# Sparse attention's queries computed with features as rows, their rotary partners fetched by transfers within SBUF, first weight tiles in halves, new shares

## The chip, the cores and the metric

The kernel runs on one core of one Trainium2 chip. The metric is the device time of one launch in microseconds (us). Before the change three runs gave a median of 1074.1 us (1072.49 to 1074.27).

## The reference, cut to what matters

Six stages follow one another on 256 tokens of 1024 features in fp32: a feed-forward network (FFN), a hybrid mixer, two FFNs, sparse attention (NSA) and a last FFN. The change touches the start of the first FFN and the projections at the head of the NSA.

```python
def swiglu(x, w_in, w_out):
    gate, up = jnp.split(x @ w_in, 2, axis=-1)
    ...

def nsa_mixer(x, positions, w_in, cmp_pos, cmp_w1, cmp_w2, w_out):
    proj = x @ w_in
    ...
    q, k_c, v_c, k_s, v_s, k_w, v_w, gates = jnp.split(proj, [int(s) for s in np.cumsum(sizes)], axis=-1)
    q = q.reshape(bsz, t_len, h, dk)
    ...
    q_rot = partial_rope(q, positions)
    k_s = partial_rope(k_s, positions)
    k_w = partial_rope(k_w, positions)
    ...
    k_cmp = compress_blocks(k_c, cmp_idx, cmp_pos[0], cmp_w1[0], cmp_w2[0])
    v_cmp = compress_blocks(v_c, cmp_idx, cmp_pos[1], cmp_w1[1], cmp_w2[1])
    ...
    s_cmp = jnp.einsum('bqged,bcgd->bgeqc', qg, k_cmp) * scale
    s_sel = jnp.einsum('bqged,bgqmd->bgeqm', qrg, k_sel) * scale
    s_win = jnp.einsum('bqged,bkgd->bgeqk', qrg, kw) * scale
    ...
    return o @ w_out
```

There are 16 heads of 64 features; the turn takes the first 16. `s_cmp` uses the plain queries, `s_sel` and `s_win` the turned ones. The rotary turn pairs feature d with feature d + 8 for d in 0 to 7 of each head: the first becomes x1 cos - x2 sin, the second x2 cos + x1 sin.

## The kernel before

**Products.** Each fp32 factor is split into a rounded half `hi` and a remainder `lo`, and each product is three matmuls (hi·hi, hi·lo, lo·hi; `mm3`). A weight tile arrives as `raw` (128x1024, 512 KB) by a DMA of the SP queue (`arrive`, L681). `split` (L672) writes `whi`, on ACT or DVE, and `wlo = raw - whi`, always on DVE. `col_tiles` (L709) gives tiles with 128 output features and all 8 blocks of 128 input features; `row_tiles` (L713) gives tiles with 512 output features and 2 input blocks.

**The order.** The program first lists all operations. `Plan.order` (L360) then sets the order on the engines by a model of their times, with each operation's place in the list as its priority; every engine works through its queue in that order. All instructions are issued by one line (L574), so the tiles' names tell them apart. In the NSA four strands are woven by `W_NSA` (L60, L2154): `attention`, `dense`, `compressed` and `out_g0`; the numbers set how fast each strand advances in the list.

**The NSA's head.** Token blocks b (2 of 128) and head groups g (2 of 8 heads). `dense` (L1930) does, for b = 0 and 1: keys, values and gates (`kv`), for b = 1 the compression's projections (`compress_in`, L1951: products `ps<-x,whi`, copies to `F`, sums to `X`), then `queries(0, wq, [b])`, then `keys(b)`, which splits the turned keys to `kd`; at the end come the queries of g = 1 for both blocks.

**The queries before** (L1885). For each g and b 24 matmuls `ps<-whi,x` or `ps<-wlo,x` of 512 columns give 128 tokens by 512 features. ACT copies them to `q`. Four fp32 transposes on PE (`mp<-ident,q`), with a copy, give the plain `qT`. `rope` turns `q` by six small operations on POOL or DVE. Four more transposes bring the turned queries to PSUM, from where `qs` is split in 64-row pieces (two CAST and two TENSOR_TENSOR on DVE for each g and b). `attend` (L2040) uses `qs`: scores `kd,qs`, the row maxima (TENSOR_REDUCE), `Exp` on ACT to `P`, a scaling of `P` (one half on DVE, one on ACT in eight pieces), transposes `mp<-ident,P`, copies to `PT`, products with `vtok`. `cmp_probs` uses `qT`. `compress` multiplies `X` by weights that are used unsplit (`mp<-raw,X`).

**The start** (`first_loads` L729, `first_steps` L1045). The tokens arrive in four DMAs of 256 KB: the first (block b = 0, first 4 input blocks) on the ACT queue, the others on SP. Weight tile 0 comes in two halves, the others whole. PE runs two warming calls on `ones`, then the products, four input blocks for b = 0 and then for b = 1.

Of the kernel before, what the change touches and what calls it, by code (L numbers as in the profile page):

```python
# [10 lines left out]
F32R = mybir.dt.float32r  # L11
# [48 lines left out]
W_HYB, W_NSA = (63.0, 66.0, 28.0, 29.0, 10.0), (81.0, 59.0, 103.0, 17.0)  # L60
# [9 lines left out]
HARD = False  # L70


def H3(t, h):
    return t.rearrange("p (h t) -> p h t", h=h)
# [118 lines left out]
class Plan:  # L193
# [83 lines left out]
    def price(self, op, eng, fn, args, kw):  # L277
# [15 lines left out]
        if fn == "dma_start":  # L293
            return {"sync": 60.0, "scalar": 400.0}.get(eng, 1100.0)
# [303 lines left out]
class K:  # L598
# [130 lines left out]
    def first_loads(self, x, w):  # L729

        nc = self.nc
        raws = []
        for n in range(8):
            raw = self.m4(1024, "raw", "W")
            if n % 2 == 0 and n < 4:
                self.first_tokens(x, n)
            for cs in [slice(0, 512), slice(512, 1024)] if n == 0 else [slice(0, 1024)]:
                nc.sync.dma_start(raw[:, cs], w[n][:, cs])
            if n % 2 and n < 4:
                self.first_tokens(x, n)  # L740
            raws.append(raw)
        return raws

    def first_tokens(self, x, n):

        queue = self.nc.sync if n else self.nc.scalar
        queue.dma_start(x[1][n // 2][:, n % 2], self.i['x_cols'][n].rearrange("p (k t) -> p k t", k=4))

    def first_weights(self, raw, parts):

        hi, lo = (self.m4(1024, name, "W", F32R) for name in ("whi", "wlo"))
        for cs in parts:
            self.split(hi[:, cs], lo[:, cs], raw[:, cs])
        return [(hi[:, k * 512:k * 512 + 512], lo[:, k * 512:k * 512 + 512]) for k in range(2)]
# [290 lines left out]
    def first_steps(self, x, w_in, gtiles, gts):  # L1045
# [6 lines left out]
        for c0, tag in ((0, "acc"), (DFF, "ps")):  # L1052
            both = [self.bank(tag) for b in range(2)]
            banks.append(both)
            w = []
            for n in range(4):
                for ks, hi, lo in self.halves(x, n % 2, n // 2) if c0 == 0 and n % 2 == 0 else []:
                    self.split(hi, lo, x[1][n // 2][:, n % 2, ks])
                w += self.first_weights(raws.pop(0), [slice(0, 1024)] if c0 or n > 1 else [slice(0, 512), slice(512, 1024)])
                for ks, hi, lo in self.halves(x, n % 2, n // 2) if c0 == 0 and n % 2 else []:  # L1060
                    self.split(hi, lo, x[1][n // 2][:, n % 2, ks])
            for k0 in range(0, KD, 4):
                for b in range(2):
# [736 lines left out]

    def tt(self, out, a, b, op):
# [16 lines left out]
    def nsa(self, x, then):  # L1818
# [3 lines left out]
        w_in = i['nsa_w_tok']  # L1822
# [58 lines left out]
        q = [self.m4(1024, f"q{b}") for b in range(2)]  # L1881
        qT = [H3(self.m4(1024, f"qT{b}"), 8) for b in range(2)]
        qs = [[H3(self.m4(1024, f"qs{b}{g}", dtype=F32R), 8) for g in range(2)] for b in range(2)]

        def queries(g, w, bs):  # L1885
            gs = slice(g * 512, (g + 1) * 512)
            for b in bs:
                ps = self.bank("ps")
                for k in range(KD):
                    self.mm3(ps, self.xb(x, b, k), w[k], k == 0, k == KD - 1)  # L1890
                    yield
                nc.scalar.activation(q[b][:, gs], ps, AF.Copy, scale=0.125)
                yield
# [5 lines left out]
                yield  # L1899
                pt = self.bank("mp")  # L1900
                for c in range(4):
                    nc.tensor.transpose(pt[:, c * P:(c + 1) * P], q[b][:, g * 512 + c * P:g * 512 + (c + 1) * P], self.ident)
                s = qs[b][g].rearrange("p (c two) t -> p c two t", two=2)
                up, dn = slice(0, 64), slice(64, 128)
                for e, (hi, lo) in enumerate(((up, dn), (dn, up))):
                    src = H3(pt, 4)[hi]
                    self.copy(s[hi, :, e, :], src)
                    V.tensor_tensor(s[lo, :, e, :], src, s[hi, :, e, :].bitcast(F32), OP.subtract)
                done.add(("q", g, b))
        kd = [self.m4(1024, f"kd{n}", dtype=F32R).rearrange("p (g r t) -> p g r t", g=2, r=2) for n in range(2)]  # L1910
# [11 lines left out]
        wq = self.row_tiles([w_in[n] for n in range(4)], 2)  # L1922
        wc = []
        done = set()
# [364 lines left out]
```

## Time and profile before

| what | us |
|---|---|
| median of three runs | 1074.1 |
| the profiled execution | 1073.94 |
| its span, first to last instruction | 1072.2 |
| the NSA's part of the span, about | 766 to 890 |
| the first product of the first FFN | 5.98 |

The profile's page gives the busy time of the engines and the chain that ended last. Its views group instructions by line and tile, give the waits of an engine, the chain in order of time, the timeline, and the busy time of each engine in chosen stretches. In a row such as `PE MATMUL mp<-ident,P`, `mp` is written and the others are read; for matmuls the tile named first is either factor. A time in brackets is the idle time ahead of a row and what ended it.

### The profile page before, as it was taken

The page shows a single profiled execution, that of the slowest core. Times are in us where ns is not written, and L with a number is a line of the kernel's source. Part 1 is how long each engine was busy: PE and PEld are TensorE (multiplying, and loading weights), DVE is VectorE, ACT ScalarE, POOL GpSimd, SP SyncE. Part 2 cuts the span into 40 slices and gives each one's busy share as a digit, 9 for nine tenths or more (in the row PEclk, how much of TensorE's full clock was granted, in tenths as well). Part 3 has the DMA queues.
Part 4 walks back from the last instruction along what each step waited for, and adds up shares of the span by engine and source line. Part 5 has one row for each costly group of instructions (what it writes and reads, how often), then busy time and mean ns, then how long its engine had stood idle before and what let it go on. Part 6 is the DMA issues. An engine that isn't in the chain of part 4 may idle for free.

```text
span 1072.2 us, 16134 instructions
## 1 busy us (share of the span) xinstructions
PE 1060.2 (99%) x5924; PEld 887.9 (83%) x5924; DVE 1010.4 (94%) x1440; ACT 724.1 (68%) x1155; POOL 76.6 (7%) x125
## 2 busy tenths in 40 slices
PE   9999999999999999999999999999999999999997
PEld 6888888898999888888888888888887778888886
DVE  6999999889969999999999999999988989999996
ACT  6678866489726766577766676677565877667770
POOL 1000000001002120000000000000011000000000
PEclk9999999999999999999999999999999999999999
DMA  9688868535515665478777647778552436467861
GB/s 367 226 274 235 254 219 289 166 131 186 182 41 179 199 232 177 142 251 244 203 240 272 225 144 237 234 248 254 204 217 67 151 114 219 151 222 236 261 191 39
DMA packets 65535, 217.79 MB, mean 203 GB/s; under 512 B 8576, under 2 KB 12336, under 8 KB 65456
## 3 DMA queue, kind: packets, MB, share of 16 engines
q1 hardware_dynamic: 60992, 200.77, 53.1%
q0 software_dynamic: 4320, 15.73, 8.2%
q8 instruction: 46, 0.75, 0.3%
q14 instruction: 33, 0.27, 0.1%
q10 hardware_dynamic: 144, 0.26, 0.1%
HBM read 213.96 MB, written 1.07 MB: 201 GB/s over the span
## 4 chain that ended last, share of the span: by engine, by line
PE 90%; DVE 6%; ACT 2%; DMA 1%; issue 1%; DVEq 0%; ACTq 0%
PE ps L574 42%; PE acc L574 33%; PE mp L574 15%; DVE wlo L574 2%; DVE arena L574 1%; DVE cv L574 1%; ACT whi L574 1%; DVE AT L574 0%; DMA raw<-in_hyb_w_tok_dram 0%; DMA X<-in_x_cols_dram 0%; DMA raw<-in_nsa_w_one_dram 0%; DVE P L574 0%; ACT cv L574 0%; DVE h L574 0%; DVE qs L574 0%
## 5 line engine op out<-in xcount | busy, mean ns | idle before, releaser
L574 DVE TENSOR_TENSOR wlo<-raw,whi 128x1024 fp32r<-128x1024 f32 (+3 forms) x417 | 490.0, 1206 | 9.9 <-ACT whi L574 8.7
L574 ACT ACTIVATE whi<-raw 128x1024 fp32r<-128x1024 f32 (+2 forms) x431 | 431.3, 1047 | 73.4 <-DVE raw L574 65.3
L574 PE MATMUL ps<-whi,x 128*128 128x512 f32 (+1 forms) x864 | 233.4, 387 | 0.0
L574 PEld LDWEIGHTS ps<-whi,x 128*128 128x128 f32 x864 | 157.2, 188 | 28.3
L574 DVE TENSOR_TENSOR raw<-raw,raw 128x1024 f32<-128x1024 f32 x128 | 152.3, 1215 | 0.0
L574 PE MATMUL ps<-wlo,x 128*128 128x512 f32 (+1 forms) x432 | 129.5, 387 | 0.0
L574 PE MATMUL ps<-x,whi 128*128 128x256 f32 (+2 forms) x560 | 115.3, 312 | 0.3 <-ACT cv L574 0.2
L574 PE MATMUL acc<-whi,gh 128*128 128x512 f32 x253 | 98.3, 392 | 0.0
L574 PE MATMUL acc<-whi,gl 128*128 128x512 f32 x253 | 98.1, 390 | 0.1
L574 PEld LDWEIGHTS ps<-x,whi 128*128 128x128 f32 (+1 forms) x560 | 90.3, 188 | 9.3 <-ACT cv L574 2.7
L574 PEld LDWEIGHTS ps<-wlo,x 128*128 128x128 f32 x432 | 79.4, 188 | 14.2 <-DVE wlo L574 0.2
L574 PE MATMUL acc<-wlo,gh 128*128 128x512 f32 x253 | 84.8, 392 | 0.0
L574 PE MATMUL ps<-x,wlo 128*128 128x256 f32 (+1 forms) x344 | 80.2, 286 | 0.0
L574 PE MATMUL acc<-whi,x 128*128 128x512 f32 x224 | 75.2, 411 | 1.1 <-ACT whi L574 1.1
L574 POOL DMA_DIRECT2D wlo<-in_ffn_w_out_dram x30 | 26.2, 873 | 558.7 <-ACT wlo L574 321.9
L574 PE MATMUL acc<-whi,g 128*128 128x512 f32 x192 | 61.2, 393 | 0.0
L574 PEld LDWEIGHTS ps<-x,wlo 128*128 128x128 f32 (+1 forms) x344 | 58.0, 189 | 1.7 <-DVE wlo L574 0.4
L574 PEld LDWEIGHTS acc<-whi,gl 128*128 128x128 f32 x253 | 47.4, 188 | 10.2 <-DVE gl L574 0.5
L574 PEld LDWEIGHTS acc<-whi,gh 128*128 128x128 f32 x253 | 47.4, 188 | 9.9 <-ACT gh L574 0.2
L574 PEld LDWEIGHTS acc<-wlo,gh 128*128 128x128 f32 x253 | 47.4, 188 | 9.7
L574 PEld LDWEIGHTS acc<-whi,x 128*128 128x128 f32 x224 | 42.3, 193 | 10.9 <-ACT whi L574 2.7
L574 PE MATMUL ps<-whi,fhi 128*128 128x512 f32 x128 | 50.0, 390 | 0.0
(287 smaller groups left out, 1722.5 us busy)
## 6 DMA issues: line engine op xcount, KB each, us to landing
raw<-in_ffn_w_in_dram SPq DMA_DIRECT2D x175, 512.0 KB, 5.3
raw<-in_ffn_w_out_dram SPq DMA_DIRECT2D x88, 512.0 KB, 4.0
wlo<-in_ffn_w_out_dram POOLq DMA_DIRECT2D x30, 512.0 KB, 7.6
raw<-in_hyb_w_col_dram SPq DMA_DIRECT2D x28, 512.0 KB, 4.6
raw<-in_hyb_w_tok_dram SPq DMA_DIRECT2D x16, 512.0 KB, 7.2
raw<-in_hyb_w_out_dram SPq DMA_DIRECT2D x16, 512.0 KB, 3.5
raw<-in_nsa_w_tok_dram SPq DMA_DIRECT2D x8, 512.0 KB, 5.4
raw<-in_nsa_w_one_dram SPq DMA_DIRECT2D x8, 512.0 KB, 5.0
```

Of the source, the lines that this page charges most:

```text
L574: r = getattr(getattr(nc, eng), fn)(*[res(a) for a in args], **{k: res(a) for k, a in kw.items()})
```

## The change

The queries' weights come by columns, as eight tiles ahead of the compression's two in one tensor (`nsa_w_col`). For each g, 96 matmuls `ps<-x,whi` or `ps<-x,wlo` of 256 columns (both token blocks) give 512 features as rows; ACT writes them to `qT` in two copies. No transposes of `q` are left. The partner feature of each turned feature lies 8 rows away: four DMAs of the SP queue per g (8 rows by 1024 columns of fp32, 32 KB each) copy those rows of `qT` to `qp`, whose other rows are zeroed once by POOL. Then `qr = qT*cos`, `qp = qp*sin`, `qr = qr + qp`, three DVE operations of 128x1024, and `qs` is split from `qr` in SBUF. `turn_tables` makes cos and sin as rows: eight small DVE operations, four memsets on POOL, four PE transposes and one copy.

The order of `dense` is now: `kv(0)`, tables, `keys(0)`, queries of g = 0 for both blocks, `kv(1)`, `keys(1)`, `compress_in`, queries of g = 1. The shares `W_NSA` are new. `LATE_IN` is False.

At the start all four token DMAs are on the SP queue, and weight tiles 0 to 2 come in halves, in the order of `FIRST`; the products of the first half of `first_steps` go input block by input block, for both token blocks. The planner's price of a DMA issued by ACT, 400 ns, is dropped.

```diff
-W_HYB, W_NSA = (63.0, 66.0, 28.0, 29.0, 10.0), (81.0, 59.0, 103.0, 17.0)
+W_HYB, W_NSA = (63.0, 66.0, 28.0, 29.0, 10.0), (786.0, 182.0, 288.0, 2.0)
...
+ALL, HALVES = slice(0, 1024), [slice(0, 512), slice(512, 1024)]
+FIRST = [("x", 0, None), ("w", 0, HALVES[0]), ("x", 1, None), ("w", 0, HALVES[1]), ("w", 1, HALVES[0]), ("w", 1, HALVES[1]),
+         ("x", 2, None), ("w", 2, HALVES[0]), ("w", 2, HALVES[1]), ("x", 3, None), ("w", 3, ALL)]
+PRODUCTS = [(k, k + 1, (0, 1)) for k in range(8)], [(k, k + 2, (0, 1)) for k in range(0, 8, 2)]
...
+    def turn_tables(self):
...
+        nc, V = self.nc, self.nc.vector
+        pt = self.bank("mp")
+        for n, t in enumerate(self.cs):
+            for b in range(2):
+                f = self.sm([P, P], f"turn{n}{b}")
+                nc.gpsimd.memset(f, 1.0 - n)
...
+                nc.tensor.transpose(pt[:, o:o + P], f, self.ident)
+        turns = self.m4(512, "turns")
+        self.copy(turns, pt)
...
-        def queries(g, w, bs):
...
-            for b in bs:
                 ps = self.bank("ps")
-                for k in range(KD):
-                    self.mm3(ps, self.xb(x, b, k), w[k], k == 0, k == KD - 1)
...
-                nc.scalar.activation(q[b][:, gs], ps, AF.Copy, scale=0.125)
...
-                pt = self.bank("mp")
-                for c in range(4):
-                    nc.tensor.transpose(pt[:, c * P:(c + 1) * P], q[b][:, g * 512 + c * P:g * 512 + (c + 1) * P], self.ident)
-                self.copy(qT[b][:, g * 4:g * 4 + 4, :], H3(pt, 4))
-                self.rope(H3(q[b][:, gs], 8), b, 8)
...
+        def queries(g, w):
+            for p in range(2):
...
+                for e in range(2):
+                    wh, wl = w[2 * p + e]
+                    for k in range(KD):
+                        self.mm3(ps[:, e * T:(e + 1) * T], (wh[:, k, :], wl[:, k, :]), self.xk(x, k),
+                                 e + k == 0, e == 1 and k == KD - 1)
...
+                nc.scalar.activation(qT[g][:, 2 * p:2 * p + 2, :], H3(ps, 2), AF.Copy, scale=0.125)
+            for r in (0, 64):
+                nc.sync.dma_start(qp[g][r:r + 8], qT[g][r + 8:r + 16])
+                nc.sync.dma_start(qp[g][r + 8:r + 16], qT[g][r:r + 8])
...
+            V.tensor_tensor(qr, qT[g], cos, OP.mult)
...
+            V.tensor_tensor(qp[g], qp[g], sin, OP.mult)
+            V.tensor_tensor(qr, qr, qp[g], OP.add)
...
         def dense():
             for b in range(2):
-                if b == 1:
-                    wc.extend(self.col_tiles([i['nsa_w_col'][n] for n in range(2)]))
                 yield from kv(b)
...
-                if b == 1:
-                    yield from compress_in()
-                yield from queries(0, wq, [b])
...
+                if b == 0:
+                    self.turn_tables()
...
                 keys(b)
...
                 self.scale_h(b)
...
+                if b == 1:
+                    if not LATE_IN:
+                        yield from compress_in()
+                else:
+                    yield from queries(0, wq)
-            yield from queries(1, self.row_tiles([w_in[4 + n] for n in range(4)], 2), range(2))
+            yield from queries(1, self.col_tiles([i['nsa_w_col'][4 + c] for c in range(4)]))
```

How this moves the instructions is shown at three places. First the SP queue at the head of the NSA, where the loads of weights are issued. Before, the queries' last tile (`in_nsa_w_tok`), the compression's two (`in_nsa_w_col`) and its unsplit ones stand in a row:

```order
L574 DMA raw_7681<-in_nsa_w_tok_dram 128x1024
L574 DMA raw_7906<-in_nsa_w_col_dram 128x1024
L574 DMA raw_7928<-in_nsa_w_col_dram 128x1024
L574 DMA raw_7960<-in_nsa_w_one_dram 128x1024
L574 DMA raw_7964<-in_nsa_w_one_dram 128x1024
```

With the change `raw_7938` and `raw_7970` are the compression's tiles, and 8004, 8050, 8065 and 8102 the queries' of g = 1:

```order
L581 DMA raw_7685<-in_nsa_w_col_dram 128x1024
L581 DMA raw_7938<-in_nsa_w_col_dram 128x1024
L581 DMA qp_1466_7847<-qT_1472_7892 8x1024 x4
L581 DMA raw_7970<-in_nsa_w_col_dram 128x1024
L581 DMA raw_8004<-in_nsa_w_col_dram 128x1024
L581 DMA raw_8050<-in_nsa_w_col_dram 128x1024
L581 DMA raw_8065<-in_nsa_w_col_dram 128x1024
L581 DMA raw_8102<-in_nsa_w_col_dram 128x1024
L581 DMA raw_8219<-in_nsa_w_one_dram 128x1024
```

The four transfers to `qp`, which read `qT`, stand ahead of the loads of one compression tile, of all tiles of the queries of g = 1 and of the unsplit weights.

Second DVE where the first `qs` is made. Before, from the transposed queries in PSUM (`mp_7867`), with the keys' remainder (`kd`) and the first maxima behind it:

```order
L574 CAST qs_1474_7875<-mp_7867 64x4x128 x2
L574 TENSOR_TENSOR qs_1474_7875<-mp_7867,qs_1474_7875 64x4x128 x2
L574 TENSOR_TENSOR kd_1480_7912<-mp_7863,kd_1475_7878 128x4x128
L574 TENSOR_REDUCE arena_7882<-acc_7819 128x4
L574 TENSOR_REDUCE arena_7882<-acc_7823 128x4
```

With the change, from `qr`; `qs_1489` is the one of b = 0, `qs_1490` that of b = 1:

```order
L581 TENSOR_TENSOR qr_1479_7953<-qT_1472_7892,turns_7861 128x1024
L581 TENSOR_TENSOR wlo_7968<-raw_7938,whi_7941 128x1024
L581 TENSOR_TENSOR qp_1466_7847<-qp_1466_7847,turns_7861 128x1024
L581 TENSOR_TENSOR qr_1479_7953<-qr_1479_7953,qp_1466_7847 128x1024
L581 TENSOR_TENSOR wlo_8015<-raw_7970,whi_8002 128x1024
L581 TENSOR_TENSOR qs_1489_8017<-qr_1479_7953,qs_1489_8017 64x4x128 x2
L581 TENSOR_TENSOR qs_1490_8028<-qr_1479_7953,qs_1490_8028 64x4x128
L581 TENSOR_REDUCE arena_7851<-acc_7943 128x4
```

The multiplication that reads `qp`, the sum and the remainder of a weight tile (`wlo_8015`) now stand ahead of the remainder of `qs`.

Third PE where the first block's probabilities `P` are transposed. Before, products of the compression (`ps_8012`) and of the queries of b = 1 (`ps_8075`) stand between the transposes of the second half, `P_7991`:

```order
L574 MATMUL ps_8012<-x_7672,whi_7930 128x256 x2
L574 MATMUL mp_8070<-ident_134,P_7991 128x128
L574 MATMUL ps_8012<-x_7672,wlo_7962 128x256
L574 MATMUL ps_8075<-whi_7631,x_7650 128x512
L574 MATMUL ps_8075<-wlo_7692,x_7650 128x512
L574 MATMUL mp_8070<-ident_134,P_7991 128x128
L574 MATMUL ps_8075<-whi_7631,x_7650 128x512
L574 MATMUL mp_8085<-raw_7960,X_7880 32x256 x4
```

With the change `ps_8186` and `ps_8197` are the queries of g = 1; `P_8080` is the first half, `P_8131` the second:

```order
L581 MATMUL ps_8109<-x_7676,wlo_8015 128x256
L581 MATMUL mp_8166<-ident_131,P_8080 128x128 x4
L581 MATMUL mp_8175<-ident_131,P_8080 128x128 x4
L581 MATMUL ps_8186<-x_7654,whi_8048 128x256 x2
L581 MATMUL mp_8191<-ident_131,P_8131 128x128
L581 MATMUL ps_8197<-x_7654,whi_8100 128x256 x2
L581 MATMUL mp_8201<-ident_131,P_8131 128x128
L581 MATMUL mp_8191<-ident_131,P_8131 128x128
L581 MATMUL mp_8201<-ident_131,P_8131 128x128
```

All other products of the compression's projections stand ahead of the transposes of `P_8080`, and four products with `whi` are the only other work among the transposes of `P_8131`; the one with the remainder of the first weight tile (`wlo_8215`) comes behind them and behind the first scores of b = 1.

More of the change, by code (lines that the diff above doesn't have):

```diff
@@ L729, in first_loads, with first_weights @@
     def first_loads(self, x, w):
[L731 to L735, printed above, removed]
-                self.first_tokens(x, n)
[L737 to L741, printed above, removed]
+        raws = {}
+        for what, n, cs in FIRST + [("w", n, ALL) for n in range(4, 8)]:
+            if what == "x":
+                self.first_tokens(x, n)
+            else:
+                raw = raws[n] = raws[n] if n in raws else self.m4(1024, "raw", "W")
+                self.nc.sync.dma_start(raw[:, cs], w[n][:, cs])
         return raws
     def first_tokens(self, x, n):
[L746 to L754, printed above, removed]
+        self.nc.sync.dma_start(x[1][n // 2][:, n % 2], self.i['x_cols'][n].rearrange("p (k t) -> p k t", k=4))
+    def first_weights(self, n, raw, cs, w):
+        if n not in w:
+            w[n] = tuple(self.m4(1024, name, "W", F32R) for name in ("whi", "wlo"))
+        for c in cs:
+            self.split(*(t[:, c] for t in (*w[n], raw)))
     def token_forms(self, x):
@@ L1898, in queries @@
-                self.rope(H3(q[b][:, gs], 8), b, 8)
[L1899 to L1902, printed above, removed]
+                for e in range(2):
[3 more added lines that the diff above has]
+                                 e + k == 0, e == 1 and k == KD - 1)
+                        yield
@@ L1903, in queries @@
+            V.tensor_tensor(qr, qr, qp[g], OP.add)
+            for b in range(2):
                 s = qs[b][g].rearrange("p (c two) t -> p c two t", two=2)
@@ L1921, in keys @@
             self.split(kd[0][:, :, :, tb], kd[1][:, :, :, tb], pt.rearrange("p (g r t) -> p g r t", g=2, r=2))
-        wq = self.row_tiles([w_in[n] for n in range(4)], 2)
         wc = []
+        wq = self.col_tiles([i['nsa_w_col'][c] for c in range(4)])
         done = set()
@@ L1941, in dense @@
                 self.scale_h(b)
[L1942 to L1943 removed]
+                if b == 1:
+                    if not LATE_IN:
+                        yield from compress_in()
+                else:
+                    yield from queries(0, wq)
+            yield from queries(1, self.col_tiles([i['nsa_w_col'][4 + c] for c in range(4)]))
+            if LATE_IN:
+                yield from compress_in()
         kcb = self.sm([P, 2, 2, 16], "kcb")
@@ L1951, in compress_in @@
         def compress_in():
+            wc.extend(self.col_tiles([i['nsa_w_col'][8 + n] for n in range(2)]))
             nc.gpsimd.memset(X[:, :, :, :, 15:16], 0.0)
@@ L2257, in laid_out @@
     w = a.pop('nsa_w_in')[0]
-    a['nsa_w_tok'] = np.concatenate([rows(w[:, c:c + 512], 2) for c in (0, 512)])
-    a['nsa_w_col'] = cols(w[:, 1024:1280])
+    a['nsa_w_col'] = cols(w[:, :1280])
     kv = np.zeros((2, 3, P, 840), np.float32)
```

61 lines of the change are left out of this document (37 added, 24 removed).

## Prediction

> **What bounds the kernel now.** I read the page first, for the engine that limits; then the waits of PE in the NSA; then the busy time in stretches, for the start and the NSA apart.
>
> ```profile
> span 1072.2 us, 16134 instructions
> ...
> PE 1060.2 (99%) x5924; PEld 887.9 (83%) x5924; DVE 1010.4 (94%) x1440; ACT 724.1 (68%) x1155; POOL 76.6 (7%) x125
> ...
> PE 90%; DVE 6%; ACT 2%; DMA 1%; issue 1%; DVEq 0%; ACTq 0%
> ```
>
> PE is busy for all but 12.0 us of the span and carries 90% of the chain that ended last. DVE is at 94%: not the bound over the whole, but close enough to become it for some microseconds. So the time moves by two things only: PE work added or taken away, and PE idle time ended or made. These are the waits of PE from 760 to 890 us, and then the stretches (core's us, then for each engine busy us and instructions, granted clock, DMA share, GB/s):
>
> ```profile
> PE mp L574 <- DVE PT L574: 0.9, 1, 0.9
> ```
> ```profile
> 5.98:10.00 4.02, 4.02 (x10) 3.15 (x11) 3.82 (x8) 3.42 (x8) 0.00 (x0) 1.00 1.01 389
> 10.00:18.65 8.65, 8.65 (x40) 7.14 (x38) 5.66 (x7) 5.63 (x8) 0.00 (x0) 1.00 1.03 413
> 770.00:800.00 30.00, 29.88 (x231) 26.94 (x229) 25.06 (x54) 19.02 (x69) 1.99 (x8) 1.00 0.65 235
> 830.00:860.00 30.00, 29.08 (x194) 21.18 (x192) 28.74 (x64) 24.76 (x82) 0.44 (x1) 1.00 0.47 159
> ```
>
> In the two stretches of the NSA in which the queries are made, 60 us, PE idles 0.12 + 0.92 = 1.04 us. There is almost no hole to fill; there is much room for new ones.
>
> **The start.** The timeline of PE and that of ACT (start, us, and in brackets the idle time ahead and what ended it):
>
> ```profile
> 1.07 3.78 PE L574 MATMUL acc<-ones 128*128 128x512 f32 x4 [1.07 <-POOL ones L574]
> 5.98 2.08 PE L574 MATMUL acc<-whi,x 128*128 128x512 f32 x4 [1.13 <-ACT whi L574]
> ```
> ```profile
> 4.69 0.72 ACT L574 ACTIVATE x<-X 128x256 fp32r<-128x256 f32 x2 [1.95 <-DMA X<-in_x_cols_dram]
> 5.32 2.33 ACT L574 ACTIVATE whi<-raw 128x512 fp32r<-128x512 f32 x4
> ```
>
> The first product waits for the tokens, then for ACT's two conversions, then for the first `whi`. The tokens, on ACT's queue, share the transfer rate with the first weights, on SP's. At 389 GB/s (the stretch from 5.98) 256 KB take 0.66 us, so tokens that go ahead on one queue land about 0.6 us sooner, and the conversions behind them move with them: I take **-0.6**. The ends are -1.13, the whole idle time of PE there, and +0.3, one issue by which the first half tile now starts later. The loads that follow cover: six products, 1.3 us at 0.216 each, for every 0.66 us of transfer.
>
> The rows also show a change of rate: 10 matmuls in the 4.02 us up to 10.00, 0.40 each, then 40 in 8.65, 0.216 each, though the column of the granted clock says 1.00 for both. If it follows the first product by 4 us, 0.6 are gained. If it stays at 10.0, the 0.6 us hold 1.5 products at 0.40 that else follow at 0.216, and 1.5 x 0.216 = 0.3 are gained. [...]
>
> **PE's work for the queries.** Rates from the timeline, 512, 280 and 256 columns; transposes from the chain of waits; their number from the tile `q`:
>
> ```profile
> 776.07 0.61 PE L574 MATMUL ps<-whi,x 128*128 128x512 f32 x2
> ...
> 776.75 0.61 PE L574 MATMUL ps<-whi,x 128*128 128x512 f32 x2
> ...
> 788.57 1.19 PE L574 MATMUL ps<-wlo,x 128*128 128x280 f32 x8
> 789.60 0.40 PE L574 MATMUL ps<-x,whi 128*128 128x256 f32 x2
> ...
> 793.18 0.40 PE L574 MATMUL ps<-x,whi 128*128 128x256 f32 x2
> ```
> ```profile
> 782.08 0.87 PE mp L574 x8
> ```
> ```profile
> L574 PE MATMUL mp<-ident,q x32: 270/272/275, 780.0 to 851.2; 128*128 128x128 f32 x32
> ```
>
> Three matmuls of 512 columns take 0.68 us: 0.227 each. Eight of 280 take 1.03: 0.129. Thirty of 256 take 3.58: 0.120. Eight transposes take 0.87: 0.109.
> - Queries: 96 x 0.227 = 21.8 becomes 192 x 0.120 = 23.0: +1.2.
> - Transposes of `q`: 32 x 0.109 = -3.5. Of the tables: 4 x 0.109 = +0.4.
> - Sum **-1.9**. The idle time of before, 1.04, was in the making of the last queries and the transposes around it, which are rebuilt: **-1.0**, with 0 as the other end.
>
> Gains in all: 0.6 + 1.9 + 1.0 = 3.5. The table's small operations, POOL's memsets and zeroings stand ahead of `keys(0)`, while PE is at the queries of g = 0 for 11.5 us; without that cover they would cost about 2, some ten pieces of 0.2 (as the RECIPROCAL below). DVE as a whole keeps its amount: six operations of 1.22 come, six CASTs of 0.69, copies and parts of the old turn go.
>
> **New wait 1, before the first scores.** Rows for it: two of DVE's groups (busy us, mean ns), ACT's copy of the queries, an issue of SP, and landings:
>
> ```profile
> L574 DVE TENSOR_TENSOR wlo<-raw,whi 128x1024 fp32r<-128x1024 f32 x18 | 22.0, 1225 | 0.3 <-issue 0.2
> ...
> L574 DVE TENSOR_TENSOR qs<-mp,qs 64x512 fp32r<-64x512 f32 x8 | 5.5, 690 | 0.3
> ```
> ```profile
> 779.21 0.60 ACT L574 ACTIVATE q<-ps 128x512 f32<-128x512 f32 x1 [2.17 <-PE ps L574]
> ```
> ```profile
> 835.95 0.33 SPq L574 DMA_DIRECT2D lng<-in_ln_g_dram  x1
> ```
> ```profile
> raw<-in_nsa_w_out_dram SPq DMA_DIRECT2D x8, 512.0 KB, 3.6
> raw<-in_nsa_w_col_dram SPq DMA_DIRECT2D x2, 512.0 KB, 4.7
> rows<-arena SPq DMA_DIRECT2D x1, 24.0 KB, 2.1
> ```
>
> Let PE end the last query product of g = 0 at 0. `qT` is copied at 0.8. SP issues four transfers to `qp`, 0.33 each, until 2.2. The trace of before has no transfer within SBUF; the nearest in size is `rows<-arena`, 24 KB in 2.1 us; the far end is 4.7, of a 512 KB tile. I take 2.1: landing at 4.0. DVE multiplies and adds, 2 x 1.22: 6.5. Next in its queue stands the remainder of the compression's second tile, whose load is issued behind the transfers, at 2.2; with 3.6 it lands at 5.8, ACT has its `whi` at 7.0 (twice the 0.58 of a half tile at the start), DVE its remainder at 8.3, and `qs`, 0.69 later, frees the scores at 9.2 with the steps between engines. PE has till then 4 x 0.227 + 48 x 0.129 + 8 x 0.120 = 8.1 us of other work in its queue. Wait: **+1.1**, from 0 (the tile lands with the transfers) to 3.1: transfers that take 4.7 move the sum to 9.1, past the tile's 7.0, and all behind it by 2.0.
>
> **New wait 2, from the first scores to the queries of g = 1.** More of DVE's groups, and two neighbouring rows of its timeline:
>
> ```profile
> L574 DVE CAST whi<-raw 128x1024 fp32r<-128x1024 f32 x4 | 2.9, 714 | 0.0
> ...
> L574 DVE RECIPROCAL arena<-arena 128x8 f32<-128x8 f32 x12 | 2.3, 195 | 1.3 <-ACT P L574 1.1
> L574 DVE TENSOR_TENSOR X<-F,arena 128x240 f32<-128x240 f32 x4 | 2.2, 568 | 0.0
> ...
> L574 DVE COPY F<-ps 64x255 f32<-64x255 f32 x4 | 1.7, 422 | 0.1
> ```
> ```profile
> 787.17 1.29 DVE L574 TENSOR_REDUCE arena<-acc 128x4 f32<-128x512 f32 x2 [0.71 <-PE acc L574]
> 788.38 2.35 DVE L574 TENSOR_TENSOR wlo<-raw,whi 128x1024 fp32r<-128x1024 f32 x2
> ```
>
> Behind the first scores DVE's queue holds, up to the first remainder of the queries of g = 1 (`wlo_8215`): 4 maxima 2.6, a CAST of a tile 0.7, a last `qs` 0.7, two operations for the second keys and a copy of `PT` (512 columns, as `qs`: 0.7 each) 2.1, the scaling of `P` 1.2 (128x1024, as `wlo`), 4 copies to `F` 1.7, 4 sums to `X` 2.3, some eight of about 0.2, 1.6, and `wlo_8215` itself 1.2: 14.1 us. Two remainders in a row take 2.35 where one takes 1.225, so neighbours overlap by 0.1; for some thirteen of them 1.3, which leaves 12.8. They begin 0.8 behind the first score (four score matmuls, 0.5, and the step to DVE), so the remainder is there at 13.6. PE's queue up to the product that reads it: 16 scores 1.9, 16 + 24 products of the compression 4.8, 4 + 16 transposes 2.2, 4 products 0.5, the next scores 1.0: 10.4. PE idles the difference, first at the transposes of `P`, then at that product: **+3.2**. The ends: 0, if DVE's pieces are ready sooner and PE's own work runs long; 5, if the durations add up without overlap and a landing holds DVE once more. Before, the queries of b = 1 and the rest of `kv(1)` stood ready in that place.
>
> At the queries of g = 1, `qp` is fetched again behind a load of output weights; scores of earlier blocks stand beside it: **+0.3** (0 to 2). Elsewhere the order differs by swaps of neighbours under a busy PE: 0 (-0.7 to +0.7).
>
> **Sum.** Against the profiled execution, 1073.94 us (1072.2 of span, 1.7 around it; 0.2 below the median): -3.5 + 1.1 + 3.2 + 0.3 = +1.1, **1075.0 us**. A measurement of this kernel tells about 0.2%, 2.1 us, from no change; this counts as none.
>
> **Rivals.**
> 1. *The new waits are mostly filled*: faster. For it: of 4.6 us of waits none is measured, each is a difference of two long sums, and before DVE waited only 1.3 us ahead of all its RECIPROCALs. If 0.8 of them are left, 1073.9 - 3.5 + 0.8 = 1071.2. Against it: in the new order the eight pieces of the second `P` stand singly with only four products among them; nothing else was ready.
> 2. *DVE's queue is held longer*: slower. From the multiplication with `qp` to `wlo_8215` DVE stands in one row of work that ends after PE's, so whatever holds it there goes into PE's idle time once. If the pieces do not overlap it is 14.1 for 12.8, +1.3; if the transfers land in 3.6, as an undisturbed tile, +0.9 more, since 0.6 of the 1.5 hide behind the tile's remainder: 1075.0 + 2.2 = 1077.2. With 4.7, 1.3 + 2.0 more, 1078.3. From 1.2 us of further delay on it is slower by more than 0.2%. For it: no cover after it, DVE at 94%. Against it: 32 KB is little data.
> 3. *The second rate comes earlier*: if the warming calls, which end 1.13 us ahead of the first product now and would end 0.5 ahead, count with the products, the ten up to 10.00 cost 0.216 for 0.40, 1.8 less: 1073.2.
> 4. *The start gives nothing* (the tokens' landing is latency, not shared rate): 1075.6.
>
> **How the numbers follow.** Forecast 0.33, its own range 1072.2 to 1076.2; rival 1 0.32; rival 2 0.28; rival 3 0.04; rival 4 0.03. Faster is rival 1: 0.32. Slower is rival 2: 0.28. Same is the rest: 0.40. The range reaches from rival 1 with no wait left and the start at its best (1073.9 - 3.5 - 0.5 = 1069.9) to rival 2 with transfers of 4.7 (1078.3).
>
> **What would show it.** Right: 192 matmuls of 256 columns, no transposes of `q`; first product near 5.4; idle PE ahead of `acc<-kd,qs`, `mp<-ident,P` and the first `ps<-x,wlo` of g = 1, 4 to 5 us in all, with DVE as the releaser; transfers to `qp` landing in about 2.1. Wrong: idle PE under 1 us there (rival 1); over 6 us (rival 2); products at 0.216 from 7 us on (rival 3); a new idle stretch outside the NSA's head, or at its end, of which nothing here speaks.

## The result and the profile after

The changed kernel takes 1080.88 us (median of five runs, 1079.69 to 1081.5) where the kernel before takes 1073.9: a ratio of 1.0066, 95% interval 1.0055 to 1.0077. It is slower by 0.66%, or 7.0 us. The forecast was 1075.0, its range ended at 1078.3.

From the page of the changed kernel, the span and the busy time of the engines:

```profile
span 1079.2 us, 16270 instructions
...
PE 1061.1 (98%) x5992; PEld 891.8 (83%) x5992; DVE 1010.7 (94%) x1436; ACT 726.8 (67%) x1162; POOL 72.2 (7%) x117
```

The span grows by 7.0 us. PE's busy time grows by 0.9, where the prediction had it fall; the rest, 6.1, is idle time of PE: 18.1 us for 12.0. Where it lies is seen in the busy time by stretches, first before, then after (us of the core, then busy us and instructions of PE, PEld, DVE, ACT, POOL, the granted clock, DMA share, GB/s):

```profile
0.00:6.50 6.50, 4.30 (x5) 1.68 (x6) 1.64 (x5) 3.25 (x6) 3.68 (x21) 1.00 0.67 227
160.00:180.00 20.00, 19.95 (x91) 16.06 (x90) 19.89 (x23) 15.84 (x18) 0.00 (x0) 1.00 0.87 310
760.00:900.00 140.00, 138.94 (x891) 110.95 (x890) 125.97 (x248) 95.64 (x267) 13.60 (x32) 1.00 0.46 155
```
```profile
0.00:6.50 6.50, 4.52 (x6) 1.47 (x6) 1.84 (x5) 3.18 (x7) 3.65 (x21) 1.00 0.68 197
160.00:180.00 20.00, 18.30 (x85) 14.85 (x84) 19.01 (x23) 14.48 (x17) 0.00 (x0) 1.00 0.88 312
760.00:900.00 140.00, 134.53 (x926) 110.94 (x925) 117.10 (x229) 94.39 (x266) 8.62 (x24) 0.98 0.43 149
```

From 760 to 900 us, the NSA and the first 10 us behind it, PE idles 5.5 us for 1.1, and the clock's column says 0.98 where it said 1.00. From 160 to 180, where the first FFN passes into the hybrid mixer, it idles 1.7 for 0.05. PE's waits over the whole of the changed kernel (releaser; us in total, times, longest):

```profile
PE acc L581 <- DVE qs L581: 2.5, 1, 2.5
PE acc L581 <- ACT gh L581: 1.7, 1, 1.7
PE acc L581 <- POOL ones L581: 1.1, 1, 1.1
PE acc L581 <- ACT x L581: 1.0, 2, 0.8
PE ps L581 <- DVE qs L581: 1.0, 1, 1.0
```

The longest is the one ahead of the first scores. The chain that leads to it can be read on three engines' timelines: SP, which issues the transfers; DVE; PE (start, us; in brackets idle time and releaser):

```profile
787.30 2.87 SPq L581 DMA_DIRECT2D qp<-qT  x4
790.28 2.59 SPq L581 DMA_DIRECT2D raw<-in_nsa_w_col_dram  x5
```
```profile
792.06 1.23 DVE L581 TENSOR_TENSOR qp<-qp,turns 128x1024 f32<-128x1024 f32 x1 [2.44 <-DMA qp<-qT]
793.33 1.23 DVE L581 TENSOR_TENSOR qr<-qr,qp 128x1024 f32<-128x1024 f32 x1
795.17 1.22 DVE L581 TENSOR_TENSOR wlo<-raw,whi 128x1024 fp32r<-128x1024 f32 x1 [0.62 <-ACT whi L581]
796.42 2.12 DVE L581 TENSOR_TENSOR qs<-qr,qs 64x512 fp32r<-64x512 f32 x3
```
```profile
797.16 3.47 PE L581 MATMUL acc<-kd,qs 128*128 128x256 f32 x16 [2.50 <-DVE qs L581]
...
810.69 1.20 PE L581 MATMUL acc<-kd,qs 128*128 128x512 f32 x2
...
812.76 0.41 PE L581 MATMUL ps<-x,wlo 128*128 128x256 f32 x1
```

Every step of the forecast's chain is there in its order: transfers, multiplication, sum, the tile's remainder, `qs`, scores. SP takes 2.87 us for four issues, 0.72 each, where the prediction took 0.33 from the issue of a load. The last transfer is issued at about 789.5 and DVE starts at 792.06: 2.6 us for the forecast's 2.1. From the copy of the queries to the landing that makes 4.8 for 3.2. These 1.6 us push the tile's load back too, and the wait of 1.1, a hole in PE's work, becomes 2.5.

The next row says something else: the sixteen scores behind the wait take 3.47 us, 0.22 each, where such products take 0.12. The busy time in stretches that are cut where the clock changes shows why (the number before the last two is the granted clock):

```profile
794.66:796.69 2.03, 0.00 (x1) 0.00 (x0) 1.49 (x2) 1.98 (x4) 0.00 (x0) 1.00 0.98 389
796.69:800.10 3.41, 2.94 (x14) 2.94 (x14) 3.17 (x5) 3.34 (x8) 1.97 (x7) 0.50 1.01 407
800.10:810.35 10.25, 9.08 (x67) 7.81 (x66) 9.81 (x23) 10.17 (x47) 0.35 (x5) 1.00 1.03 413
810.35:813.76 3.41, 3.41 (x11) 2.39 (x11) 3.38 (x6) 2.65 (x4) 0.00 (x0) 0.50 1.00 370
```

After the idle time PE's granted clock falls to half for 3.4 us, twice. Half of the busy time in them, 1.5 us for the first and 1.7 for the second, is 3.2 us, an estimate of what the lower clock costs; how much of it reaches the end is read from e3 below. The prediction had priced a wait at its length.

At the start the first product comes at 4.98 (5.98 before), and products run at 0.23 from 6.55 on, where before that rate began at 10.0:

```profile
4.98 0.73 PE L581 MATMUL acc<-whi,x 128*128 128x512 f32 x2
6.55 0.50 PE L581 MATMUL acc<-whi,x 128*128 128x512 f32 x1 [0.83 <-ACT x L581]
```

The first transposes of `sg` come at 28.0 us for 29.8 before. In this execution the lead is lost again at the end of the first FFN, where ACT waits for a weight tile of the mixer and makes `su` and `gh` behind it:

```profile
168.87 1.06 ACT L581 ACTIVATE whi<-raw 128x1024 fp32r<-128x1024 f32 x1 [1.59 <-DMA raw<-in_hyb_w_tok_dram]
169.84 0.58 ACT L581 ACTIVATE su<-ps 128x512 f32<-128x512 f32 x1
170.31 0.59 ACT L581 ACTIVATE gh<-mp 128x512 fp32r<-128x512 f32 x1
```
```profile
170.96 0.73 PE L581 MATMUL acc<-whi,gh 128*128 128x512 f32 x2 [1.71 <-ACT gh L581]
```

### The profile page after: what moved, and what is told of

It reads as the page before. It is cut to its first block, busy times and chain, and to the rows that moved or that the text cites. A ratio compares the mean times of both kernels' runs of the same rounds, so it can differ in the third digit from the quotient of the medians.

```text
span 1079.2 us, 16270 instructions
## 1 busy us (share of the span) xinstructions
PE 1061.1 (98%) x5992; PEld 891.8 (83%) x5992; DVE 1010.7 (94%) x1436; ACT 726.8 (67%) x1162; POOL 72.2 (7%) x117
## 4 chain that ended last, share of the span: by engine, by line
PE 86%; DVE 6%; ACT 4%; DMA 2%; issue 1%; SPq 0%; DVEq 0%; ACTq 0%
PE ps L581 41%; PE acc L581 32%; PE mp L581 13%; DMA raw<-in_hyb_w_tok_dram 1%; ACT whi L581 1%; DVE wlo L581 1%; DVE cv L581 1%; DVE arena L581 1%; ACT P L581 1%; DVE o L581 1%; DMA X<-in_x_cols_dram 0%; DVE AT L581 0%; DMA raw<-in_nsa_w_col_dram 0%; ACT cv L581 0%; DVE h L581 0%
## 5 line engine op out<-in xcount | busy, mean ns | idle before, releaser
L581 DVE TENSOR_TENSOR wlo<-raw,whi 128x1024 fp32r<-128x1024 f32 (+2 forms) x418 | 490.9, 1207 | 8.0 <-ACT whi L581 7.1
L581 PE MATMUL ps<-whi,x 128*128 128x512 f32 (+1 forms) x800 | 210.4, 385 | 0.0
L581 PEld LDWEIGHTS ps<-whi,x 128*128 128x128 f32 x800 | 145.4, 188 | 26.4
L581 PE MATMUL ps<-x,whi 128*128 128x256 f32 (+2 forms) x688 | 141.0, 308 | 1.0 <-DVE F L581 0.4
L581 PEld LDWEIGHTS ps<-x,whi 128*128 128x128 f32 (+1 forms) x688 | 110.8, 188 | 11.6 <-ACT cv L581 2.8
L581 PE MATMUL ps<-wlo,x 128*128 128x512 f32 (+1 forms) x400 | 116.3, 385 | 0.0
L581 PE MATMUL ps<-x,wlo 128*128 128x256 f32 (+1 forms) x408 | 98.5, 286 | 0.3 <-DVE wlo L581 0.3
L581 PEld LDWEIGHTS ps<-wlo,x 128*128 128x128 f32 x400 | 72.9, 188 | 13.1 <-DVE wlo L581 0.2
L581 PEld LDWEIGHTS ps<-x,wlo 128*128 128x128 f32 (+1 forms) x408 | 70.2, 189 | 2.1 <-DVE wlo L581 0.7
```

What stands on the lines that cost most here:

```text
L581: r = getattr(getattr(nc, eng), fn)(*[res(a) for a in args], **{k: res(a) for k, a in kw.items()})
```

## The experiments

Four groups ran beside one another: e1 to e4, e5 to e8, e9 to e11, e12 to e14. Each ratio is against the kernel before in the same group (medians of 1073.1 to 1074.2 us). Differences in the text are these ratios times 1074 us, since the medians of the groups differ.

| | what | median us | ratio, 95% interval |
|---|---|---|---|
| e1 | before, with the new start | 1073.74 | 0.9994 (0.9985 to 1.0002) |
| e2 | after, with the old start | 1080.38 | 1.0052 (1.0040 to 1.0065) |
| e3 | after, no transfers | 1074.68 | 1.0009 (1.0000 to 1.0019) |
| e4 | after, PE kept busy ahead of the scores | 1080.11 | 1.0056 (1.0038 to 1.0075) |
| e5 | after, every second transfer issued by ACT | 1078.30 | 1.0047 (1.0032 to 1.0062) |
| e6 | after, the tile's split behind `qs` | 1082.06 | 1.0082 (1.0065 to 1.0098) |
| e7 | after, transfers on ACT, planned | 1083.13 | 1.0096 (1.0080 to 1.0112) |
| e8 | after, the old shares | 1086.40 | 1.0119 (1.0104 to 1.0135) |
| e9 | after, copies for transfers, same order | 1080.90 | 1.0069 (1.0056 to 1.0081) |
| e10 | copies, order chosen anew | 1072.58 | 0.9990 (0.9980 to 1.0000) |
| e11 | copies, another such order | 1072.87 | 0.9991 (0.9982 to 1.0000) |
| e12 | transfers, priced 700 ns, order chosen anew | 1076.94 | 1.0034 (1.0024 to 1.0045) |
| e13 | after, no transfers for g = 0 | 1076.62 | 1.0027 (1.0016 to 1.0037) |
| e14 | copies planned, old choice of order | 1081.40 | 1.0066 (1.0051 to 1.0080) |

### The start: e1 and e2

The edit of e1 puts the new lists and the functions that use them into the kernel before; e2 takes them out of the changed one.

```diff
+FIRST = [("x", 0, None), ("w", 0, HALVES[0]), ("x", 1, None), ("w", 0, HALVES[1]), ...]
...
-        queue = self.nc.sync if n else self.nc.scalar
-        queue.dma_start(x[1][n // 2][:, n % 2], ...)
+        self.nc.sync.dma_start(x[1][n // 2][:, n % 2], ...)
```

> The kernel before with the new start alone (order of the first loads, halved tiles, products input block by input block). Theory A, the start's gain is given back: in the changed kernel PE is 1.8 us ahead at the first transposes of sg (28.00 for 29.76) and level again at 172 us, behind a wait of 1.7 us for gh, since ACT's queue holds a tile that has not landed yet. Then this kernel takes 1073.4 to 1074.2. Rival: the give-back belongs to something else, and the start is worth its 1.8 us: about 1072.1.

> The changed kernel with the start of before. Theory A (the start's gain is given back before 172 us): 1080.4 to 1081.4, as the changed kernel. Rival (the start is worth 1.8 us): about 1082.7.

With the new start alone `sg` comes at 27.3 us, 2.5 earlier than before, and the ratio is 1 within its interval: -0.6 us, from -1.6 to +0.2. The old start in the changed kernel loses 5.6 us for 7.0; if the new one were worth its 1.8 us, that would be 8.8. So the start gains 2 us early on and little at the end, and the runs don't settle its sign. In the profiled execution of e1 PE waits 0.8 us for `gh` at that place, as in e2; e1's span of 1070.8 us is at the lower end of its eleven runs and is not taken as a gain. How much is given back differs between executions: the same product in the FFN ahead of the NSA, PE's 4251st, comes at 756.16 us before and at 756.69 in the changed kernel. In the NSA the first product with `fixed` comes at 777.7 in e1 where it comes at 779.0 before; with the new code for the queries it comes at 786.4 in the changed kernel, at 785.2 in e3, and at 786.8 in e2, which has the old start. That the loads of the mixer's weights set the time at the end of the first FFN, so that PE's lead only makes it wait longer, is read from the row of ACT above and was not tried by an experiment.

### The transfers: e3 and e13

In e3 the eight transfers are left out, so that the partner's term is missing from the turned queries; in e13 only the four of g = 0. Nothing else moves.

```diff
-    order = plan.order(...)
+    order = [o for o in plan.order(...) if not is_fetch(o)]      # e13: and not for qp of g = 0
```

> The changed kernel, every instruction in the same order, with the eight transfers to qp left out: the queries are then turned without the partner's term (qp stays zero). Theory B, the transfers hold DVE's queue and SP's loads, and the hole in front of the first scores costs more than its length: the first scores need not wait (2.5 us), are made at 0.12 us each in place of 0.21 (1.4), and the wait for the second fetch goes (1.0): about 1076. Rival: the time comes from the new order of the strands (PE starving between first scores and the queries of g = 1): at most 1 us less, about 1080.

> The changed kernel without the four transfers of g = 0 (their term is missing from the turned queries of the first eight heads); those of g = 1 stay; same order. A (the first fetch holds the head: 3.7 us of idle time and 3.1 us of a lower rate of PE): within 1.5 us of the run without any fetch, 1074.5 to 1076.3. Rival (the second fetch, at 842, costs as much as the first): 1077 to 1079.

Without transfers 6.1 us of the loss go and 1.0 stays, so Theory B holds with more than its forecast of 1076; without the first four 4.2 go, so that the second four cost 1.9 (e13's time lies between its two forecasts). The head of the NSA on PE in e3, from the scores to the first product with the remainder of g = 1:

```profile
793.30 2.08 PE L581 MATMUL acc<-kd,qs 128*128 128x256 f32 x16
...
801.35 1.06 PE L581 MATMUL mp<-ident,P 128*128 128x128 f32 x8 [0.74 <-ACT P L581]
803.21 0.50 PE L581 MATMUL ps<-x,whi 128*128 128x256 f32 x2 [0.80 <-ACT F L581]
...
804.55 2.08 PE L581 MATMUL mp<-ident,P 128*128 128x128 f32 x7
...
807.53 0.28 PE L581 MATMUL ps<-x,wlo 128*128 128x256 f32 x1
```

The scores start at 793.30, so the remainder is used 14.2 us later; the forecast was 13.6. PE idles 0.7 + 0.8, and the seven transposes that take 2.08 where eight took 1.06 hide another 1.2 us in gaps too short to be listed: 2.7 in all, for 3.2 forecast. The second new wait was priced about right, and even without the first the kernel only draws level with the one before.

PE's matmuls are the same in e3 and in the changed kernel, in the same order, so the start of each can be compared (us, from the two timelines):

| PE's matmul | e3 | changed kernel | later by |
|---|---|---|---|
| last product ahead of the first scores | 793.07 | 794.26 | 1.2 |
| first score | 793.30 | 797.16 | 3.9 |
| first product behind the scores | 795.22 | 800.46 | 5.2 |
| first scores of b = 1 (512 columns) | 806.39 | 810.69 | 4.3 |
| first product with `vtok` | 808.41 | 814.07 | 5.7 |
| end of the span | 1072.4 | 1079.2 | 6.8 |

Of the 1.2 us ahead of the head 0.9 come from the wait for `gh`, which e3's execution doesn't have. The hole costs 2.7, the slow scores 1.4. Behind them PE waits 0.9 less for the other engines, because it comes later; the second slow stretch costs 1.4, and the second fetch 1.1. So PE's lower rate costs 1.4 + 1.4 = **2.7 us** (1.38 + 1.36), somewhat less than the 3.2 of the clock's column. These are two single executions; the medians differ by 6.1.

### The rate: e4

Eighteen products of zeros stand ahead of the first scores, where PE would idle.

```diff
+    order[first:first] = [("tensor", "matmul", (out, zr, r), dict(start=False, stop=False))] * 18
```

> The changed kernel with 18 products by a tile of zeros put into PE's queue just ahead of the first scores, adding nothing to an open sum; they fit in the 2.5 us in which PE idles there. Theory C, the idle time itself lowers PE's rate behind it (granted clock 0.50 from 798 to 800): the 16 scores are made at 0.12 us each again, 1.4 us less, about 1079.5, and the granted clock stays at 1.00 there. Rival: the scores are slow for another reason, or the rate falls with waits that the zeros do not change: 1080.9, clock as before.

The scores now take 2.17 us for 3.47 and the clock holds there (1.00 from 796 to 800), so in this pair of executions the lower rate goes with the idle time. The whole gains 1.1 us, which the intervals don't separate from none: the clock falls ten us later instead, after idle stretches of 1.0 and 0.8 us (stretches of e4 from 802 on), and its mean from 760 to 900 is 0.98, as in the changed kernel:

```profile
802.00:804.00 2.00, 1.24 (x11) 1.03 (x9) 2.00 (x4) 2.00 (x14) 0.00 (x0) 1.00 1.03 420
804.00:806.00 2.00, 1.07 (x8) 0.86 (x8) 1.87 (x8) 1.95 (x9) 0.00 (x0) 1.00 1.03 416
806.00:808.00 2.00, 1.96 (x8) 1.36 (x8) 1.96 (x6) 1.96 (x6) 0.00 (x0) 0.56 1.03 410
808.00:810.00 2.00, 2.00 (x9) 1.46 (x8) 2.00 (x3) 2.00 (x6) 0.00 (x0) 0.58 1.03 410
```

e3 idles 0.7 + 0.8 us at the same place and its clock stays at 1.00. So it isn't the length of the idle time alone that decides; e12 below has the clearest case.

### The way the transfers are issued: e5, e6, e7; the shares: e8

e5 gives every second transfer to ACT's queue, in the same order; e7 gives all to it and lets the planner, which is told 700 ns for each, arrange the rest; e6 moves the split of the compression's tile behind the first `qs`; e8 puts the old `W_NSA` back.

```diff
-    nc.sync.dma_start(qp[g][r:r + 8], qT[g][r + 8:r + 16])
+    nc.scalar.dma_start(qp[g][r:r + 8], qT[g][r + 8:r + 16])                 # e5 (every second), e7
...
-W_HYB, W_NSA = ..., (786.0, 182.0, 288.0, 2.0)
+W_HYB, W_NSA = ..., (81.0, 59.0, 103.0, 17.0)                                # e8
```

> The changed kernel in the same order, with every second transfer to qp issued by ACT in place of SP. Theory B1, the four issues of 0.72 us each in a row are the largest part of the hold: the last issue of the first fetch ends 1.4 us sooner, the tile behind it lands as much sooner, PE idles 1.1 us ahead of the first scores for 2.5 (and 0.3 for 1.0 ahead of those after the second fetch), and the rate may then stay: 1077 to 1079. Rival, the transfers' own flight of about 2.6 us or DVE's queue sets the wait: 1080.5 to 1081.

> The changed kernel with the halves of the tile that is loaded behind the fetch (whi on ACT, wlo on DVE) put behind the first qs, the rest in the same order. Theory B2, this tile stands in the way of qs: scores 1.0 us sooner, PE idles 1.5 for 2.5: 1079 to 1080. Rival, qs waits for the sum qr alone: no change, 1080.9.

> The changed kernel with the fetch on ACT's queue, at a price of 700 ns for each in the planner, which then orders the rest anew: all loads are issued without waiting for qT, and 18 more products of the compression stand ahead of the first scores. Theory B: the hole ahead of the scores goes (2.5 and 1.4 of lower rate), the queries of g = 1 have their tiles in time: 1074 to 1076. Rival, DVE's sum of work is the bound and the hole only moves behind the scores: 1079 to 1081.

> The changed kernel with the shares of before (81, 59, 103, 17). Theory B: the SP queue and the place of the first scores are the same as with the new shares, so the hole is too: 1080 to 1082. Rival, the new shares make the loss: 1076 or less.

e5 cuts the wait ahead of the scores to 1.4 us, and gains 2.0 us, as Theory B1 forecast (the intervals overlap a little); the scores run at the full rate (2.18 us for the sixteen), but behind them the clock's mean from 800 to 820 is 0.83, which makes an estimate of 6.8 us at half; the products are slower from 805 on. In e6 that wait falls to 1.3 as well, but its theory missed: the hole moves to the transposes of `P` and is longer there (its waits):

```profile
PE mp L581 <- DVE P L581: 3.9, 1, 3.9
PE acc L581 <- DVE qs L581: 1.3, 1, 1.3
```

The remainder that was put back now waits 2.4 us for `whi`, and the maxima and `P` stand behind it on DVE. e7 is slower than both of its forecasts: the scores still wait 2.2 us for `qs`, and at the second fetch three issues, of 0.63 us in the median, stand ahead of the scaling of `P` on ACT, for which PE waits 2.4. e8 says that the new shares aren't the loss: the new code with the old ones is 5.7 us slower still, which neither of its forecasts had.

### Copies in place of the transfers: e9, e14, e10, e11; transfers in a new order: e12

The weight columns of the queries and of the turned keys are laid out so that the partner lies 32 rows away, and an engine copies it, 32 rows by 512 columns at a time (0.63 us on ACT and 0.42 on DVE in e9), eight copies for each g. In e9 six of them are put on ACT and two on DVE, and all else keeps its order; in e14 the planner places them. e10 and e11 are e14 with shares and shifts of the order that were chosen anew for it. e12 keeps the transfers, but charges SP 700 ns for an issue (60 before), and has its order chosen anew too.

```diff
-            for r in (0, 64):
-                nc.sync.dma_start(qp[g][r:r + 8], qT[g][r + 8:r + 16])
-                nc.sync.dma_start(qp[g][r + 8:r + 16], qT[g][r:r + 8])
+                for r in (0, 32, 64, 96):
+                    self.copy(qp[g][r:r + 32, 2 * p:2 * p + 2, :], qT[g][r ^ 32:(r ^ 32) + 32, 2 * p:2 * p + 2, :])
...
+    turn = np.r_[0:8, 16:40, 8:16, 40:64]
+    w[:, c:c + 64] = w[:, c + turn]
...
+    4: [(386, 8.0, 8)],   W_NSA = (511.0, 93.0, 180.0, 9.0)      # e10
+    4: [(770, 8.0, 8)],   W_NSA = (812.0, 93.0, 207.0, 11.0)     # e11
+    4: [(35, 5.0, 8)],    W_NSA = (786.0, 195.0, 288.0, 2.0)     # e12
```

> The changed kernel, complete, without the transfers: the weight columns of the queries and of the turned keys are laid out so that the rotary partner lies 32 rows away instead of 8, and an engine can copy it (32 rows by 512 columns; for each g four copies on ACT behind the first copy of the queries, then two on ACT and two on DVE behind the second). All other instructions keep their order. Theory A (the loss is the chain of four transfers ahead of the first scores and what follows from it): like the run without the fetch, with up to 1 us more for two copies that stand on DVE ahead of the sum: 1074.2 to 1076.0 where the kernel before is 1073.9; idle PE ahead of the first scores under 0.8; their clock 1.0, 0.13 each. Rival (part of what the run without the fetch gained was the missing work itself: any way to fetch the partner delays DVE's queue, and PE loses it): 1077.5 to 1080.

> As the version with copies in place of transfers, but the copies are part of the planned program, and the four shares of the NSA and the small shifts of the order are chosen anew for it (511, 93, 180, 9). A (the order of the changed kernel was chosen for transfers that were priced too low; with the queries' saved PE work of 1.9 us, and without the second wait of about 3 us, the rewritten queries are faster than the kernel before): 1070.5 to 1073. Rival (the wait behind the first scores comes from DVE's queue, which a new order only moves): 1073.5 to 1076.

> The same with another choice of shares and shifts (812, 93, 207, 11). Same numbers as for the run with the first choice; what differs between the two shows how much of such a gain hangs on one choice.

> The changed kernel with its transfers, but the planner charges SP 700 ns for issuing one (the traces show 0.72 us; it charged 60 ns), and the shares and shifts of the NSA's order are chosen anew for that (786, 195, 288, 2, other shifts). A (the copies between partitions were what made a better order possible: four issues and a landing of 2.6 us take 5.5 us of every order): 1075 to 1079. Rival (the order, not the way the partner is fetched, is what the two runs with copies and a new order gained): 1072 to 1074.5.

> Copies in place of transfers, placed by the planner (on ACT or DVE, whichever it finds free), with the shares and shifts of the changed kernel. A (fixed places on ACT were what cost the version with copies; placing them by the planner is enough): 1073 to 1076. Rival (this choice of shares and shifts has no room for the copies anywhere, and only choosing them anew brings the gain): 1077 to 1082.

e9 went against the theory that e3 had seemed to show. The transfers are gone, the scores start at 793.43 as in e3, and the kernel is as slow as with them. Where it loses is another place: at the first product with the remainder of g = 1 (808.48) e9 is 1.0 us behind e3, where the changed kernel is 5.2 behind, and at the end 6.1. So at the head the copies cost little, as its Theory A said, and some 5 us are lost at the second fetch, where the transfers cost 1.1. ACT and then PE in e9, at the second fetch, and the stretches there:

```profile
829.77 2.55 ACT L581 ACTIVATE qp<-qT 32x512 f32<-32x512 f32 x4
832.35 1.06 ACT L581 ACTIVATE whi<-raw 128x1024 fp32r<-128x1024 f32 x1
833.31 0.89 ACT L581 ACTIVATE P<-P,arena 128x256 f32<-128x256 f32 x2
```
```profile
833.86 0.44 PE L581 MATMUL mp<-ident,P 128*128 128x128 f32 x2 [2.16 <-ACT P L581]
```
```profile
834.00:836.00 2.00, 2.00 (x13) 1.90 (x13) 1.27 (x2) 1.91 (x7) 0.00 (x0) 0.73 0.00 0
836.00:838.00 2.00, 2.00 (x11) 1.82 (x10) 0.00 (x0) 1.54 (x4) 0.00 (x0) 0.50 0.02 4
```

Four copies of 0.64 us and a `whi` stand ahead of the scaling of `P` in ACT's queue, PE waits 2.2 for it, and the clock falls to half again (0.50 from 836 to 838). At the head of the NSA, with idle time of 1.2 + 0.8, the clock falls too, to 0.55 and 0.60 in the two stretches from 804 to 808. e14 shows that placing the copies by the planner isn't enough either. With a new order the same copies cost nothing that can be measured: e10 and e11 stand 1.1 and 1.0 us below the kernel before, which counts as no change (their intervals reach to 1.0000), so the gain that Theory A forecast for them isn't shown. PE's waits of e10 in the NSA, all that are listed from 760 to 900, and its page:

```profile
PE mp L581 <- DVE PT L581: 0.9, 2, 0.5
PE ps L581 <- DVE F L581: 0.8, 1, 0.8
```
```profile
PE 1057.3 (99%) x5992; PEld 889.0 (83%) x5992; DVE 1013.1 (95%) x1443; ACT 731.7 (68%) x1171; POOL 70.2 (7%) x115
```

The number of matmuls is that of the changed kernel, 5992, and PE is busy 3.8 us less. In e12, with transfers and a new order, 3.4 us of the loss go and 3.7 stay. Its PE has one long wait, for a remainder on DVE; the row, the stretches around it, and the page:

```profile
805.76 0.38 PE L581 MATMUL ps<-x,wlo 128*128 128x256 f32 x1 [2.01 <-DVE wlo L581]
```
```profile
804.00:806.00 2.00, 0.24 (x2) 0.24 (x3) 2.00 (x5) 2.00 (x13) 0.00 (x0) 1.00 1.04 422
806.00:808.00 2.00, 2.00 (x18) 2.00 (x18) 2.00 (x5) 1.98 (x11) 0.00 (x0) 1.00 1.02 410
```
```profile
PE 1058.0 (99%) x5992; PEld 889.7 (83%) x5992; DVE 1010.5 (94%) x1438; ACT 727.7 (68%) x1164; POOL 74.7 (7%) x115
```

PE idles 2.0 us without a break and goes on at the full clock. With the same 5992 matmuls as the changed kernel it is busy 3.1 us less. Not all of that need be the clock: gaps too short to be listed count as busy too, 1.2 us of them in e3, whose clock stays at 1.00 from 760 to 900; so busy time alone doesn't price the clock. Neither way of fetching the partner is free in the order that was timed, and both get cheaper in another. How much of the 4.7 us between e12 and e10 is the transfers' own and how much the luck of one choice of order stays open, since only one order was tried with transfers at their right price. Nor was the price tried apart from the new choice of shares.

## Why the prediction was wrong, step by step

The span grew by 7.0 us where the sum had 1.1 more. By its terms, measured in the profiled executions of before, e3 and the changed kernel:

| term | forecast | measured |
|---|---|---|
| start, up to the NSA | -0.6 | +0.5 in this execution (-0.7 in e3, -1.3 in e1) |
| PE's work, the old idle time and new wait 2: -1.9 - 1.0 + 3.2 | +0.3 | +0.9 in e3; in the changed kernel 0.9 less |
| new wait 1 | +1.1 | +2.7 (2.5 of it listed) |
| PE's lower rate behind the waits | none | +2.7 |
| the second fetch | +0.3 | +1.1 |
| sum | +1.1 | +7.0 |

- **The step that failed** is the price of a wait: "PE idles the difference". The prediction used the clock at the start of the program, and nowhere else. Nearly half of the loss that it missed, 2.7 of 5.9 us, is PE at half its clock behind two holes. The clock's column shows it (0.50), the comparison with e3 prices it, and e4's scores, 2.17 us for 3.47 with products in place of the idle time, tie it to the idle time.
- **New wait 1** was the right mechanism with a term mis-sized: 2.5 us for 1.1. An issue of a transfer of 8 rows within SBUF takes 0.72 us for 0.33, and a transfer 2.6 for 2.1. The row of `rows<-arena` was a fair neighbour for the landing; the issue of one load of `lng` was no neighbour for four transfers in a row. One issue takes 0.72 us beside a flight of 2.6, and four in a row, 2.87, take longer than the flight.
- **New wait 2** was about right (13.6 us forecast, 14.2 in e3). In the changed kernel it hardly shows as idle time, because PE came late, and behind it worked at half the clock: 0.3 + 0.2 + 0.2 + 0.4 us of waits from 806 to 809, and the slow rows at 810.69 and 812.76.
- **The second fetch** was put at 0.3 and costs 1.1 in the profiled executions, nearly all of it the wait `ps <- DVE qs` of 1.0, and 1.9 by the medians (e13 against e3).
- **The start**: the first tokens land 2.8 us after their issue where they took 3.9 beside the first weights, and the first product comes 1.0 us sooner for the forecast's 0.6. The second rate came as rival 3 had it, from 6.5 us on; that the warming calls bring it was rival 3's assumption and was not shown. PE led by 1.8 us at 28 us. That such a lead reaches the end was rival 3's tacit step, and e2 refutes it. The forecast's own -0.6 lies within e1's interval, as 0 does.
- **Rival 2**, DVE's queue held longer, came nearest: it named the place and the direction, and its top, 1078.3, fell short by 2.6 us, about what the rate took. That these two agree is luck, since the start and the second fetch were off too.

A wrong turn of the study itself: e3 had seemed to settle that the transfers cost 6 us and that any other fetch would save them. e9 refuted the second half. At the head, where the transfers cost most, its copies cost little; in the same order they cost as much at the second fetch. What the runs bear out is narrower: in this order each fetch that was tried, on SP, on SP and ACT, or on ACT and DVE, makes PE wait 1 to 2.5 us at one or two places, and behind some of these waits PE's clock was at half for 3.4 us (the changed kernel, e9).

## What to carry to other kernels

Where an engine is busy for 99% of the span, price a new wait at its length and, beside it, at the 1.4 us that PE's half clock added here behind each of two holes; look for that in the clock's column of short stretches, since PE counts as busy there (3.41 us of 3.41 in the second). An edit that is right in its own sum can still lose when the order around it was chosen with a wrong price for one instruction (60 ns for 0.72 us here): set the price first, choose the order anew, and then judge the edit. Leaving a piece out shows what it costs in this place, not what a replacement will cost.

## What the hardware showed that was not expected

- The granted clock was at half for 3.4 us after idle time of 2.5 us (after), of 2.2 us (e9), of 1.0 + 0.8 us (e4) and even of 1.2 us in four pieces (after, ahead of 810), and for 6.8 us in e5 (for e4, e9 and e5 worked out from the means of stretches). It did not fall after 2.0 us without a break (e12) or 0.7 + 0.8 us (e3). Each of these is one execution. So the length of a hole alone doesn't decide; what does, no run here shows.
- Whether the clock falls may also differ between executions of one kernel, which is not shown: the ten runs of e12 take 1075.57 to 1079.81 us at mean clocks of 0.996 to 0.999, the fastest, which is the traced one, at 0.999, but the slowest at 0.997; the eleven of e10, which has no wait over 0.8 us in the NSA, take 1072.19 to 1075.0 at 0.997 to 0.999.
- A transfer of 32 KB from 8 rows of SBUF to 8 others costs SP 0.62 to 0.80 us to issue, and ACT 0.80 in the mean of four (e7), more than the 0.33 of the load of `lng` (before), which brings 512 KB.
- A copy of 32 rows by 512 columns takes 0.63 us on ACT and 0.42 on DVE (e10). On ACT a copy of 128 rows costs as much (`qT` from PSUM, 128x512: 0.60, after).
